# Six weight slots in two sizes, down halves behind the fifth product, a norm shift from three tiles

## The chip, the cores and the metric

The kernel runs on one core of a Trainium2 chip. Its engines are named as in the profile: PE (TensorE matmul; PEld is its weight load), DVE (VectorE), ACT (ScalarE), POOL (GpSimd) and SP (SyncE, which issues nearly all DMAs here). The metric is device time of one launch in microseconds. Before the change it is 1253.96 us, the median of three runs (1253.59 to 1255.86).

## The reference, cut to what matters

Two request groups (a prompt of 512 positions and a sample of 32) go through two layers that share their weights, 544 columns in all; the model is 1024 wide.

```python
for l in range(DEPTH):                       # 2 layers
    z = x @ w_in                             # one projection, split among three mixers
    a = gmlp(z); b = latent_attention(z); c = rg_lru(z)
    x = layer_norm(ALPHA * x + concat(a, b, c) @ w_o)        # first norm
    up = x @ w_up                            # 1024 -> 2 * 2816
    g, v = split(causal_dwconv3(up))
    x = layer_norm(ALPHA * x + (gelu(g) * v) @ w_down)       # second norm
```

All of it is fp32, and the caches and states are outputs too.

## The kernel before

**Layout and arithmetic.** Activations lie transposed: eight tiles `xT` of 128 features by 544 columns. Each product is made of three fp32r matmuls (lines 88 to 91): both operands are split into a high part (ACT rounds it) and a low part (DVE subtracts it), and high x high, high x low and low x high are summed. A PSUM bank holds half the columns, 272, so every product runs in two halves `hv`.

**Weights.** A raw weight tile is loaded by SP into one of four slots `wr` (line 94), and split into a high and a low tile in the slots `wh` and `wl`, five of each, 1024 columns wide (lines 102 to 112, and `pair` in `forms`). Some tiles next to a norm go to pages of 512 columns instead (`page_weights`, line 223). A split can't start before a slot is free, and a slot is free when the last matmul on its tile has run.

**Stages of a layer.** The mixer projects with tiles of w_in: latent weights in three tiles `wkv`, then `wuqr`, two gate tiles `wga0` and `wga1`, and so on (lines 330 to 470). `wo_stage` runs w_o's eight tiles through `proj_ln`: the tiles 0 and 1 together, then one by one; for the last three both halves are put apart, and the first two up tiles are split to slots meanwhile (`pre_up`, line 1039), so that the norm's first half can be done while PE runs the last second halves.

**The feed-forward** (`ffn`, line 1086) has 22 units, each a gate tile and a value tile of 128 features, in four column blocks `BLK` of 6, 4, 5 and 7 units. In the first block a unit is two plain projections, 96 matmuls. The other blocks use seven products of half size in place of eight (`seven`, line 1147), 84 matmuls a unit: the differences of the activations are the four pairs `TX`, made once by `mixed_x` while the first block runs (`settle`, line 1094), those of the weights are made for each unit by `forms` (line 1047): splits A11 and A12 (`fa`), S3 and S1 (`fb`), S2 and S4 (`fc`), each 1024 columns, and A22 (`fd`), 512. The gated result of a unit is split into two pages whose pool `FPT` names by block and unit: `g` for pages `pg`, `p` for `pp`, `t` for `pt`.

**Down products.** After each block its part of w_down runs: eight tiles, two halves each, 16 halves. For the first three blocks these are the generator `late`, and the next block pulls from it: `seven` stops after its second and after its fifth product, and the halves of that unit are shared between the two places (lines 1200 to 1207). A tile's weights are loaded and split when its first half is pulled. The last block's down product runs in `proj_ln` with the second norm.

**The norm** (`LN`, line 842) shifts by a mean before squaring: when the first four tiles are summed into `lns`, PE sums over partitions (line 886), ACT copies the mean, DVE subtracts it from all eight tiles, and the squares of tiles 1 to 3 are added in the shift, those of later tiles as they arrive. `stats` and `apply` then make the normed tiles, half by half; for the kernel's last norm four tiles are put apart instead of three, and the output is stored from there.

**Order.** The program is written as one sequence; a planner puts each engine's instructions in order ahead of the launch, by its own estimate of when operands and slots are there, and adds the semaphores. Engines then run their queues in that order.

Of the kernel before, what the change touches and what calls it, by code (L numbers as in the profile page):

```python
# [8 lines left out]
F32R = mybir.dt.float32r  # L9
AF = mybir.ActivationFunctionType  # L10
ALU = mybir.AluOpType
# [8 lines left out]
HW = 272  # L20
# [2 lines left out]
PG = 550  # L23
D_FF = 2816
NI = 22
BLK = ((0, 6), (6, 4), (10, 5), (15, 7))
FPT = ("", "ggpp", "", "ggppp")
KO = (0, 2, 4, 6, 1, 3, 5, 7)
ALPHA = (2.0 * DEPTH) ** 0.25
SCALE = 96 ** -0.5  # L30
# [16 lines left out]
def trunk_kernel(ctx: ExitStack, tc: tile.TileContext, i, o, k):  # L47
# [1 line left out]
    pool = ctx.enter_context(tc.tile_pool(name="sb", bufs=1))  # L49
    psum = ctx.enter_context(tc.tile_pool(name="ps", bufs=1, space=bass.MemoryType.PSUM))  # L50
    dram = ctx.enter_context(tc.tile_pool(name="dr", bufs=1, space=bass.MemoryType.DRAM))
    BUFS = dict(pg=28, pt=12, kb=8, pp=8, wr=4, wh=5, wl=5)

    def page(name, dt=F32, tag="pg"):
        return pool.tile([128, W if tag == "pp" else PG], dt, tag=tag, name=name, bufs=BUFS[tag])
# [38 lines left out]
    def load_w(src, kk, cols, name):  # L94
        wr = pool.tile([128, kk, cols], F32, tag="wr", name=name + "r", bufs=BUFS["wr"])
        nc.sync.dma_start(out=wr, in_=src)
        return wr
# [1 line left out]
    def raw_page(name):  # L99
        return pool.tile([128, 512], F32, tag="wr", name=name, bufs=BUFS["wr"])  # L100

    def split_w(wr, kk, cols, name):
        wh = pool.tile([128, kk, cols], F32R, tag="wh", name=name + "h", bufs=BUFS["wh"])
        wl = pool.tile([128, kk, cols], F32R, tag="wl", name=name + "l", bufs=BUFS["wl"])
        with ExitStack() as st:
            for ins in gate:
                st.enter_context(tc.issue_after(ins.ins))
            split(wh, wl, wr)
        return wh, wl

    def weights(src, kk, cols, name):
        return split_w(load_w(src, kk, cols, name), kk, cols, name)

    def rsqrt(y, v, t):
        a = act(y, v, AF.Abs_reciprocal_sqrt)
# [95 lines left out]
        return [[b[:, 0:HW] for b in r] for r in bs]  # L211


    def col_weights(src, kk, name, kper=8):
        res = []
        for c in range(0, kk, kper):
            n = min(kper, kk - c)
            wh, wl = weights(src[:, 128 * c:128 * (c + n)].rearrange("p (k c) -> p k c", k=n), n, 128, name)
            for j in range(n):
                res.append((wh, wl, j))  # L220
        return res
# [618 lines left out]


    class LN:
        def __init__(self, xT, first_op, va, cg, cb, spill, final, ns, tag):
            self.x, self.op, self.va, self.cg, self.cb = xT, first_op, va, cg, cb
            self.spill = spill
            self.final = final
            self.n1 = 8 - ns
            self.tag = tag

        def warm(self):  # L850
            t = const([128, 1], F32, "warm")
# [16 lines left out]
        def gather(self, m, c):  # L868
            if m == 0:
                return  # L870
            if m == 1:
                self.s = page("lns", tag=self.tag)[:, 0:W]
                tt(self.s, self.x[0][:, 0:W], self.x[1][:, 0:W], ALU.add)
                return
            s = self.s[:, c]
            tt(s, s, self.x[m][:, c], ALU.add)
            if m >= 4:
                self.square(m, c)

        def shift(self):  # L880
            s = self.s
            c = self.c = page("lnc", tag=self.tag)[:, 0:W]
            q = self.q = page("lnq", tag=self.tag)[:, 0:W]
            for h in HV:
                b = bank("lnm", "ss")
                nc.tensor.matmul(b[:, 0:HW], ones, s[:, h], start=True, stop=True)
                act(c[:, h], b[:, 0:HW], AF.Copy, scale=1.0 / 512)
            for m in (4, 0, 1, 2, 3, 5, 6, 7):
                x = self.x[m][:, 0:W]
                tt(x, x, c, ALU.subtract)  # L890
                if m == 0:
                    act(q, x, AF.Square)
                elif m in (1, 2, 3):
                    self.square(m, slice(0, W))
            stt(s, c, -4.0, s, ALU.mult, ALU.add)

        def square(self, m, c):
            t = page("lnt", tag="kb")[:, c]
# [66 lines left out]

    def proj(wsrc, kts, evac, name):
        for m in range(8):
            w = col_weights(wsrc(m), len(kts), f"{name}{m}")
            for hv in range(2):
                evac(m, hv, mms([w], kts, hv)[0])  # L970
                yield

    def proj_ln(wsrc, kts, ln, name, kper, pre, mid, ko=None):
        n1 = ln.n1
        ns = 8 - n1

        def get(m):
            w = col_weights(wsrc(m), len(kts), f"{name}{m}", kper)
            return [w[j] for j in ko] if ko else w

        for ms in ((0, 1), (2,), (3,)):
            ws = [get(m) for m in ms]
            for hv in range(2):
                for m, ps in zip(ms, mms(ws, kts, hv)):
                    ln.evac(m, hv, ps)
            if ms[0] == 0 and mid is not None:
                mid()
        def one(m, w, hv):
            ps = mms([w], kts, hv)[0]
            if m == 4 and hv == 0:  # L990
                ln.shift()
            ln.evac(m, hv, ps)

        for m in range(4, n1):
            w = get(m)
            for hv in range(2):
                one(m, w, hv)
        ws = [get(m) for m in range(n1, 8)]
        nxt = pre() if pre is not None else None
        for j in range(ns):  # L1000
            one(n1 + j, ws[j], 0)
            if j == 0:
                ln.warm()
        for j in range(ns):
            ps = mms([ws[j]], kts, 1, (lambda: ln.stats(0)) if j == 0 else ln.head if ln.final and j == ns - 1 else None, 5)[0]
            if j == 0 and not ln.final:
                ln.apply(0, range(4))
            ln.evac(n1 + j, 1, ps)
        if ln.final:
            ln.stats(1)  # L1010
            ln.apply(0)
        else:
            ln.apply(0, range(4, 8))

        def hook():
            if not ln.final:
                ln.stats(1)
            ln.apply(1)
        rest = [] if ln.final else [lambda m=m: ln.settle(m) for m in range(8)]
        return nxt, hook, rest  # L1020

    def wo_stage(l, va, pre):
        xT = []
        for m in range(8):
            x = page(f"xT{m}")
            nc.sync.dma_start(out=x[:, 0:W], in_=xd[l][m])
            if m >= 4:
                act(x[:, 0:W], x[:, 0:W], scale=ALPHA)
            xT.append(x)
        ln = LN(xT, "alpha", va, C_LN1G, C_LN1B, None, False, 3, "pp")  # L1030
        ko = [6, 7, 2, 3, 0, 4, 1, 5]

        kts = [KX[m] for m in ko]
        return xT, *proj_ln(lambda m: i["wo"][l, m], kts, ln, "wo", 8, pre, None, ko)
# [12 lines left out]
    def forms(l, i_):  # L1047
        w = [load_w(i["wup"][l, NI * s + i_].rearrange("p (k c) -> p k c", k=8), 8, 128, "wup") for s in range(2)]
        (a11, a12), (a21, a22) = [(r[:, 0:4, :], r[:, 4:8, :]) for r in w]

        def pair(n):
            return [pool.tile([128, n, 128], F32R, tag=t, name=f"wf{t}", bufs=BUFS[t]) for t in ("wh", "wl")]

        fa, fb, fc, fd = pair(8), pair(8), pair(8), pair(4)
        split(*fa, w[0])
        split(*fd, a22)
        tt(a22, a21, a22, ALU.add)
        tt(a21, a11, a21, ALU.subtract)
        tt(a11, a22, a11, ALU.subtract)
        tt(a12, a12, a11, ALU.subtract)  # L1060
        split(*fb, w[1])
        split(*fc, w[0])
        return dict(A11=(fa, 0), A12=(fa, 4), A22=(fd, 0), S3=(fb, 0), S1=(fb, 4), S2=(fc, 0), S4=(fc, 4))
# [22 lines left out]
    def ffn(l, va, vf, xT, first, hook, rest, pre):  # L1086
# [14 lines left out]
        for bl, (i0, nk) in enumerate(BLK):  # L1101
# [95 lines left out]
            if bl == 0:  # L1197
                for tl in tiles[done:]:
                    unit(tl)
            for j in range(nk if bl else 0):  # L1200
                mix = seven(i0 + j)
                n = 16 * (j + 1) // nk - 16 * j // nk
                for c in ((n + 1) // 2, n // 2):
                    next(mix)
                    for _ in range(c):
                        next(late)
                next(mix, None)
# [3 lines left out]

            if bl < len(BLK) - 1:
                def ev2(m, hv, ps, bl=bl):
                    x = xT[m][:, HV[hv]]
                    if bl == 0:
                        stt(x, x, ALPHA, ps, ALU.mult, ALU.add)
                    else:
                        tt(x, x, ps, ALU.add)
                late = proj(wsrc, [fts[j] for j in sorted(fts)], ev2, "wd")
            else:  # L1220
                fin = l == DEPTH - 1

                def mid():
                    nc.sync.dma_start(out=o[7][l], in_=fo)

                ln = LN(xT, "add", va, C_LN2G, C_LN2B, o[0] if fin else xd[l + 1], fin, 4 if fin else 3, "pg")
                nxt = proj_ln(wsrc, [fts[j] for j in sorted(fts)], ln, "wd", 8, pre, mid)
        return nxt

# [134 lines left out]
```

## Time and profile before

| | us |
|---|---|
| median of three runs | 1253.96 |
| the profiled execution | 1253.95 |
| its span, first to last instruction | 1252.1 |
| PE busy | 1223.2 (98%) |
| DVE busy | 1013.6 (81%) |
| ACT busy | 741.4 (59%) |
| mean granted TensorE clock | 0.995 |

Matmuls are pipelined and their ends are modelled, so PE's busy share says little of its pace; the distance between two starts does. "Idle before" is the time an engine stood still ahead of an instruction, with what ended it. The chain that ended last is PE for 82% of the span, DVE for 8% and ACT for 7%.

### The profile page before, as it was taken

The page shows a single profiled execution, that of the slowest core. Times are in us where ns is not written, and L with a number is a line of the kernel's source. Part 1 is how long each engine was busy: PE and PEld are TensorE (multiplying, and loading weights), DVE is VectorE, ACT ScalarE, POOL GpSimd, SP SyncE. Part 2 cuts the span into 40 slices and gives each one's busy share as a digit, 9 for nine tenths or more (in the row PEclk, how much of TensorE's full clock was granted, in tenths as well). Part 3 has the DMA queues.
Part 4 walks back from the last instruction along what each step waited for, and adds up shares of the span by engine and source line. Part 5 has one row for each costly group of instructions (what it writes and reads, how often), then busy time and mean ns, then how long its engine had stood idle before and what let it go on. Part 6 is the DMA issues. An engine that isn't in the chain of part 4 may idle for free.

```text
span 1252.1 us, 24029 instructions
## 1 busy us (share of the span) xinstructions
PE 1223.2 (98%) x9305; PEld 1178.7 (94%) x9305; DVE 1013.6 (81%) x1932; ACT 741.4 (59%) x1616; POOL 45.7 (4%) x222
## 2 busy tenths in 40 slices
PE   9999999999999999999899999999999999999994
PEld 9999879999999999999899997899999999999994
DVE  6766977997788889886886767689968788898858
ACT  6485874496455655553465767646955455565633
POOL 2400000000000000000000100000000000000000
PEclk9999999999999999999999999999999999999998
DMA  8243434022232332325144423340213223323312
GB/s 284 75 141 98 125 104 161 18 86 72 73 110 83 95 98 89 100 77 170 46 147 136 118 85 113 118 136 18 94 60 105 65 93 93 106 83 106 114 36 73
DMA packets 51043, 125.16 MB, mean 100 GB/s; under 512 B 7784, under 2 KB 13928, under 8 KB 50928
## 3 DMA queue, kind: packets, MB, share of 16 engines
q1 hardware_dynamic: 50928, 123.62, 31.8%
q8 instruction: 73, 1.20, 0.4%
q14 instruction: 42, 0.34, 0.1%
HBM read 113.17 MB, written 5.97 MB: 95 GB/s over the span
## 4 chain that ended last, share of the span: by engine, by line
PE 82%; DVE 8%; ACT 7%; issue 1%; DMA 0%; SPq 0%; ACTq 0%; DVEq 0%
PE mm L89 22%; PE mm L90 21%; PE mm L91 21%; ACT wfwh L64 2%; PE ov L255 2%; DVE xT L70 2%; ACT ac L64 1%; PE ol L255 1%; PE pT L132 1%; ACT xp L64 1%; DVE ac L70 1%; PE s L89 1%; DVE wupr L67 1%; DVE xT L67 1%; PE kv L396 1%
## 5 line engine op out<-in xcount | busy, mean ns | idle before, releaser
L64 ACT ACTIVATE wfwh<-wupr 128x1024 fp32r<-128x1024 f32 (+1 forms) x128 | 121.7, 951 | 122.6 <-PE mm L90 66.1
L67 DVE TENSOR_TENSOR wfwl<-wupr,wfwh 128x1024 fp32r<-128x1024 f32 (+1 forms) x128 | 139.4, 1089 | 14.3 <-ACT wfwh L64 13.0
L89 PE MATMUL mm<-th,wfwh 128*128 128x272 f32 x512 | 148.4, 291 | 0.0
L90 PE MATMUL mm<-tl,wfwh 128*128 128x272 f32 x512 | 147.4, 288 | 0.0
L91 PE MATMUL mm<-th,wfwl 128*128 128x272 f32 x512 | 146.4, 288 | 0.0
L70 DVE SCALAR_TENSOR_TENSOR ac<-xp,vf,ac 128x544 f32<-128x544 f32 x176 | 136.1, 781 | 8.0 <-ACT xp L64 7.2
L90 PE MATMUL mm<-xl,wfwh 128*128 128x272 f32 x384 | 111.1, 289 | 0.0
L91 PE MATMUL mm<-xh,wfwl 128*128 128x272 f32 x384 | 111.1, 289 | 0.0
L89 PE MATMUL mm<-xh,wuph 128*128 128x272 f32 x384 | 109.5, 291 | 1.5 <-DVE xT L67 1.5
L89 PE MATMUL mm<-xh,wfwh 128*128 128x272 f32 x384 | 110.9, 289 | 0.0
L90 PE MATMUL mm<-xl,wuph 128*128 128x272 f32 x384 | 110.3, 289 | 0.0
L91 PE MATMUL mm<-xh,wupl 128*128 128x272 f32 x384 | 110.3, 288 | 0.0
L89 PEld LDWEIGHTS mm<-th,wfwh 128*128 128x128 f32 x512 | 96.3, 188 | 1.2 <-ACT u L64 0.8
L90 PEld LDWEIGHTS mm<-tl,wfwh 128*128 128x128 f32 x512 | 96.6, 189 | 0.0
L91 PEld LDWEIGHTS mm<-th,wfwl 128*128 128x128 f32 x512 | 96.3, 189 | 0.0
L67 DVE TENSOR_TENSOR wupr<-wupr 128x512 f32<-128x512 f32 x128 | 88.2, 689 | 2.4
L89 PEld LDWEIGHTS mm<-xh,wuph 128*128 128x128 f32 x384 | 71.7, 188 | 2.3 <-DVE xT L67 1.9
L91 PEld LDWEIGHTS mm<-xh,wfwl 128*128 128x128 f32 x384 | 72.4, 189 | 0.0
L90 PEld LDWEIGHTS mm<-xl,wuph 128*128 128x128 f32 x384 | 72.4, 189 | 0.0
L89 PEld LDWEIGHTS mm<-xh,wfwh 128*128 128x128 f32 x384 | 72.4, 188 | 0.0
L90 PEld LDWEIGHTS mm<-xl,wfwh 128*128 128x128 f32 x384 | 72.3, 188 | 0.0
L91 PEld LDWEIGHTS mm<-xh,wupl 128*128 128x128 f32 x384 | 72.3, 188 | 0.0
(517 smaller groups left out, 4006.9 us busy)
## 6 DMA issues: line engine op xcount, KB each, us to landing
wupr<-in_wup_dram SPq DMA_DIRECT2D x88, 512.0 KB
xT<-in_x_dram SPq DMA_DIRECT2D x14, 272.0 KB
xd<-xT SPq DMA_DIRECT2D x8, 272.0 KB
xT<-xd SPq DMA_DIRECT2D x8, 272.0 KB
out_dram<-xT SPq DMA_DIRECT2D x16, 136.0 KB
ckT<-in_ckT_dram SPq DMA_DIRECT2D x8, 256.0 KB
cr<-in_ck_dram SPq DMA_DIRECT2D x8, 256.0 KB
win0r<-in_win_dram SPq DMA_DIRECT2D x8, 192.0 KB
```

The source lines that it names most:

```text
L64: return nc.scalar.activation(out=out, in_=in_, func=func, **kw)
L67: return (e or nc.vector).tensor_tensor(out=out, in0=a, in1=b, op=op)
L70: return nc.vector.scalar_tensor_tensor(out=out, in0=a, scalar=s, in1=b, op0=op0, op1=op1)
L89: nc.tensor.matmul(ps, lh, rh, start=start, stop=False, **kw)
L90: nc.tensor.matmul(ps, lh, rl, start=False, stop=False, **kw)
L91: lastmm[0] = nc.tensor.matmul(ps, ll, rh, start=False, stop=stop, **kw)
L132: nc.tensor.transpose(out, in_, ident[0:p, 0:p])
L255: nc.tensor.matmul(ps, a, b, start=start, stop=stop)
L396: nc.tensor.matmul(b[0:n, 0:288], XL[j][:, cs], wh[:, ci, :], start=False, stop=False)
```

## The change

The column blocks become 5, 5, 5 and 7 units. The five slots `wh`, `wl` become four (tag `w`), and two slots `vh`, `vl` of 640 columns are added (tag `v`): for A22 and for the down tiles of the first three blocks. Pages `pp` go from eight to seven, and the fifth unit of the second block keeps its result in `pt`. In the late blocks one half is pulled after the second product and the others after the fifth; the number of halves up to a unit's end is odd, but for the last. The second norm's shift is taken from the first three tiles, the first norm's still from four.

```diff
-BLK = ((0, 6), (6, 4), (10, 5), (15, 7))
-FPT = ("", "ggpp", "", "ggppp")
+BLK = ((0, 5), (5, 5), (10, 5), (15, 7))
+FPT = ("", "ggppt", "", "ggppp")
-    BUFS = dict(pg=28, pt=12, kb=8, pp=8, wr=4, wh=5, wl=5)
+    BUFS = dict(pg=28, pt=12, kb=8, pp=7, wr=4, wh=4, wl=4, vh=2, vl=2)
-    def split_w(wr, kk, cols, name):
-        wh = pool.tile([128, kk, cols], F32R, tag="wh", name=name + "h", bufs=BUFS["wh"])
-        wl = pool.tile([128, kk, cols], F32R, tag="wl", name=name + "l", bufs=BUFS["wl"])
+    def split_w(wr, kk, cols, name, tag="w"):
+        wh, wl = [pool.tile([128, kk, cols], F32R, tag=tag + p, name=name + p, bufs=BUFS[tag + p]) for p in "hl"]
...
-            if m >= 4:
+            if m >= self.n0:
                 self.square(m, c)
...
-                act(c[:, h], b[:, 0:HW], AF.Copy, scale=1.0 / 512)
-            for m in (4, 0, 1, 2, 3, 5, 6, 7):
+                act(c[:, h], b[:, 0:HW], AF.Copy, scale=1.0 / (128 * n0))
+            for m in (n0, *range(n0), *range(n0 + 1, 8)):
...
-                elif m in (1, 2, 3):
+                elif m < n0:
                     self.square(m, slice(0, W))
-            stt(s, c, -4.0, s, ALU.mult, ALU.add)
+            stt(s, c, -float(n0), s, ALU.mult, ALU.add)
...
     def proj(wsrc, kts, evac, name):
-            w = col_weights(wsrc(m), len(kts), f"{name}{m}")
+            w = col_weights(wsrc(m), len(kts), f"{name}{m}", tag="v")
...
-        for ms in ((0, 1), (2,), (3,)):
+        n0 = ln.n0
+        for ms in ((0, 1), (2,), (3,))[0:n0 - 1]:
...
-            if m == 4 and hv == 0:
+            if m == n0 and hv == 0:
                 ln.shift()
...
-        for m in range(4, n1):
+        for m in range(n0, n1):
...
         def pair(n):
-            return [pool.tile([128, n, 128], F32R, tag=t, name=f"wf{t}", bufs=BUFS[t]) for t in ("wh", "wl")]
+            w = "v" if n == 4 else "w"
+            return [pool.tile([128, n, 128], F32R, tag=w + p, name=f"wf{p}", bufs=BUFS[w + p]) for p in "hl"]
...
+            halves = 0
             for j in range(nk if bl else 0):
                 mix = seven(i0 + j)
-                n = 16 * (j + 1) // nk - 16 * j // nk
-                for c in ((n + 1) // 2, n // 2):
+                end = 16 if j == nk - 1 else 2 * round(8 * (j + 1) / nk - 0.5) + 1
+                for c in (1, end - halves - 1):
                     next(mix)
+                    halves += c
                     for _ in range(c):
                         next(late)
```

With these counts a unit's two pulls are 1 and 2, 1 and 3, 1 and 1, 1 and 3, 1 and 2 halves in a block of five units; in the block of seven they are 1 and 2 in the first and the last unit and 1 and 1 between.

## Rows read from the trace of the kernel before

**Rows 1.** The page's busy line of PE: busy us, share, instructions.
```profile
PE 1223.2 (98%) x9305; PEld 1178.7 (94%) x9305; DVE 1013.6 (81%) x1932; ACT 741.4 (59%) x1616; POOL 45.7 (4%) x222
```
**Rows 2.** Stretches: length; busy of PE, PEld, DVE, ACT, POOL (count); clock; DMA; GB/s.
```profile
207.30:226.00 18.70, 18.70 (x147) 18.54 (x147) 18.62 (x33) 10.40 (x18) 0.10 (x1) 1.00 0.39 134
233.00:307.25 74.25, 73.52 (x582) 73.12 (x581) 67.07 (x120) 56.99 (x137) 1.16 (x12) 1.00 0.19 61
307.25:386.00 78.75, 78.64 (x626) 78.40 (x625) 60.41 (x90) 39.40 (x77) 0.69 (x7) 1.00 0.26 78
465.10:572.10 107.00, 105.98 (x831) 104.51 (x830) 94.28 (x141) 63.97 (x136) 1.84 (x17) 1.00 0.34 102
```
**Rows 3.** PE's waits: what waited, for what; total us, times, longest.
```profile
PE mm L89 <- ACT wd3h L64: 1.8, 4, 0.6
...
PE mm L89 <- ACT wd2h L64: 0.6, 2, 0.3
```
**Rows 4.** Order of time in the last block: start, us, engine, instruction [idle before].
```profile
482.75 0.29 PE L91 MATMUL mm<-xh,wfwl 128*128 128x272 f32 x1
483.36 0.39 PE L89 MATMUL mm<-fh,wd1h 128*128 128x272 f32 x1 [0.32 <-ACT wd1h L64]
...
483.71 0.29 PE L89 MATMUL mm<-th,wfwh 128*128 128x272 f32 x1
...
482.77 0.33 SPq L96 DMA_DIRECT2D wd2r<-in_wdn_dram  x1
...
497.45 0.73 ACT L64 ACTIVATE wd2h<-wd2r 128x640 fp32r<-128x640 f32 x1
...
499.28 0.82 DVE L67 TENSOR_TENSOR wd2l<-wd2r,wd2h 128x640 fp32r<-128x640 f32 x1
```
**Rows 5.** Order of time at layer 0's second norm: DVE, ACT, DVE, PE.
```profile
589.79 1.08 DVE L67 TENSOR_TENSOR wd7l<-wd7r,wd7h 128x896 fp32r<-128x896 f32 x1
...
597.43 1.28 ACT L64 ACT_TABLE_LOAD   x1
...
599.34 3.27 DVE L67 TENSOR_TENSOR xT<-xT,lnc 128x544 f32<-128x544 f32 x5 [3.08 <-ACT lnc L64]
...
616.57 0.29 PE L91 MATMUL mm<-fh,wd7l 128*128 128x272 f32 x1
620.78 0.40 PE L89 MATMUL mm<-xh,win0h 128*128 128x272 f32 x1 [3.92 <-ACT xh L64]
```
**Rows 6.** Stretches at the same place, columns as in rows 2.
```profile
599.34:620.78 21.44, 17.52 (x137) 17.08 (x135) 21.24 (x46) 8.29 (x18) 0.00 (x0) 1.00 0.16 42
621.10:624.40 3.30, 3.30 (x16) 3.06 (x15) 3.30 (x10) 2.18 (x5) 0.00 (x0) 0.50 0.00 0
```
**Rows 7.** Order of time at the kernel's end: DVE, PE, DVE.
```profile
1216.75 3.27 DVE L67 TENSOR_TENSOR xT<-xT,lnc 128x544 f32<-128x544 f32 x5 [4.21 <-ACT lnc L64]
...
1236.16 0.47 PE L908 MATMUL ln<-lns,ones 128*128 128x272 f32 x1 [1.94 <-DVE lns L67]
...
1242.52 4.62 DVE L70 SCALAR_TENSOR_TENSOR xT<-xT,va,lnc 128x272 f32<-128x272 f32 x11
```
**Rows 8.** Order of time at layer 0's first norm: DVE, then PE's first up product.
```profile
202.42 1.22 DVE L67 TENSOR_TENSOR wo7l<-wo7r,wo7h 128x1024 fp32r<-128x1024 f32 x1
203.55 1.29 DVE L67 TENSOR_TENSOR wupl<-wupr,wuph 128x512 fp32r<-128x512 f32 x2
...
220.18 1.21 DVE L67 TENSOR_TENSOR wupl<-wupr,wuph 128x1024 fp32r<-128x1024 f32 x1
...
226.95 0.79 DVE L70 SCALAR_TENSOR_TENSOR xT<-ln,xT 128x272 f32<-128x272 f32 x2 [0.89 <-ACT lnt L64]
...
233.04 0.41 PE L89 MATMUL mm<-xh,wuph 128*128 128x272 f32 x2
```
**Rows 9.** Order of time at layer 0's gate tiles: PE, DVE.
```profile
53.51 0.29 PE L91 MATMUL mm<-xh,wga0l 128*128 128x272 f32 x1
...
54.98 1.21 DVE L67 TENSOR_TENSOR wga1l<-wga1r,wga1h 128x1024 fp32r<-128x1024 f32 x1
```

More of the change, by code (lines that the diff above doesn't have):

```diff
@@ L109, in split_w, with weights @@
         return wh, wl
-    def weights(src, kk, cols, name):
-        return split_w(load_w(src, kk, cols, name), kk, cols, name)
+    def weights(src, kk, cols, name, tag="w"):
+        return split_w(load_w(src, kk, cols, name), kk, cols, name, tag)
     def rsqrt(y, v, t):
@@ L211, in first_units, with col_weights @@
         return [[b[:, 0:HW] for b in r] for r in bs]
-    def col_weights(src, kk, name, kper=8):
+    def col_weights(src, kk, name, kper=8, tag="w"):
         res = []
@@ L217, in col_weights @@
             n = min(kper, kk - c)
-            wh, wl = weights(src[:, 128 * c:128 * (c + n)].rearrange("p (k c) -> p k c", k=n), n, 128, name)
+            wh, wl = weights(src[:, 128 * c:128 * (c + n)].rearrange("p (k c) -> p k c", k=n), n, 128, name, tag)
             for j in range(n):
@@ L842, in trunk_kernel, with __init__ @@
     class LN:
-        def __init__(self, xT, first_op, va, cg, cb, spill, final, ns, tag):
+        def __init__(self, xT, first_op, va, cg, cb, spill, final, ns, tag, n0):
             self.x, self.op, self.va, self.cg, self.cb = xT, first_op, va, cg, cb
@@ L848, in __init__ @@
             self.tag = tag
+            self.n0 = n0
         def warm(self):
@@ L876, in gather @@
             tt(s, s, self.x[m][:, c], ALU.add)
-            if m >= 4:
+            if m >= self.n0:
                 self.square(m, c)
         def shift(self):
-            s = self.s
+            s, n0 = self.s, self.n0
             c = self.c = page("lnc", tag=self.tag)[:, 0:W]
@@ L1029, in wo_stage @@
             xT.append(x)
-        ln = LN(xT, "alpha", va, C_LN1G, C_LN1B, None, False, 3, "pp")
+        ln = LN(xT, "alpha", va, C_LN1G, C_LN1B, None, False, 3, "pp", 4)
         ko = [6, 7, 2, 3, 0, 4, 1, 5]
@@ L1224, in mid @@
                     nc.sync.dma_start(out=o[7][l], in_=fo)
-                ln = LN(xT, "add", va, C_LN2G, C_LN2B, o[0] if fin else xd[l + 1], fin, 4 if fin else 3, "pg")
+                ln = LN(xT, "add", va, C_LN2G, C_LN2B, o[0] if fin else xd[l + 1], fin, 4 if fin else 3, "pg", 3)
                 nxt = proj_ln(wsrc, [fts[j] for j in sorted(fts)], ln, "wd", 8, pre, mid)
```

## The prediction

> **What bounds the kernel now.** I read the page's busy line first, then the stages by stretches, then PE's waits, then the engines in order of time around each wait. PE is busy for 98% of the span [rows 1], so what isn't fewer matmuls must be a wait of PE or the tail. The stretches of layer 0 [rows 2] give the pace: the column block of 307.25 to 386.00 runs 626 matmuls in 78.75 us, 0.126 each, and nearly no wait; VectorE (DVE) fills 60.4 of it, but 94.3 of 107 us in the last block. PE's waits name the rest. The weights of the down halves hold it ten times (five per layer, wd3 four times, the others two each); the first and the last of the four groups are in [rows 3], and all four sum to 4.4 us, counted from the modelled end of the matmul before. By starts one such wait costs more: 482.75 to 483.71 is three steps and takes 0.96, where three take 0.375 [rows 4], so 0.59. Six of the ten cost that, three 0.83 and one 1.05 by their starts: 7.1 us. Beside these there are two norm stalls: at the layer boundary PE starts nothing from 616.57 to 620.78 [rows 5], and runs at half clock (0.50, the 1.2 GHz level) for 3.3 us soon after [rows 6]; at the end it waits 1.94 us, and DVE then works until 1247.1 [rows 7]. The sum below stands on the profiled execution: 1253.95 us, 1.85 outside its span, and 0.01 from the median of the runs.
>
> **The change part by part.**
>
> *Column 5 by seven products.* A gated unit costs 2 tiles x 2 halves x 8 x 3 = 96 matmuls in the first block and 7 x 4 x 3 = 84 in the others. One unit per layer moves: 2 x 12 = 24 fewer, at 0.125 us: **-3.0 us**. The down products stay 22 units x 48 in all. ScalarE and DVE get one and a half more splits and four 512-column differences for it; these run beside PE. Block 0 loses two tiles (12 us of PE, and on DVE two splits, four taps, a product and a split), and keeps all four mixed pairs. DVE was busy there for 67.1 of 74.25 us [rows 2], so it gets tighter; its slack is at the block's end, where the new first forms fall. I take 0; without this cover it costs up to one split per form set, three of 1.2 us each (as wo7's, [rows 8]), 3.7 per layer; below nothing it can't go, as nothing there waits on block 0 now.
>
> *Down halves.* Now one half runs after the second product, and it is nearly always the second half of a tile whose weights are there; the others come after the fifth product, three products (36 matmuls, 4.5 us) later. So the split needn't be ready behind A11, where the waits are. The load isn't late: wd2's was issued at 482.77, its split ran at 497.45 for 0.73 us and the low part at 499.28 for 0.82 [rows 4]; SP's queue issues the same loads, cut from 768 and 512 columns to 640. What is late next: with two slots of 640, one is A22's until the seventh product. Where the second of two tiles is begun in the same unit as the first is ended (three times each in the first two late blocks, once in the last: 14 in all), its split waits for the half just run or for A22. Ends: -7.1 when no wait is left; 0 as the most that simply isn't recovered (beyond that is a rival). The order on PE already puts `th,wfwh` products between pieces of a half [rows 4], which covers one split; I take the nearer end, less 0.15 us for each of the 14: **-5.0**.
>
> *Norm shift after three tiles (second norm of a layer).* Mean, copies and subtractions start one tile of down products earlier: 42 matmuls, 5.2 us. The count of subtractions, squares and sums stays. Layer boundary: DVE stood idle for 3.08 us until 599.34, as an ACT table load of 1.28 falls between the two copies of the mean [rows 5], and from there DVE is full until PE restarts [rows 6]. Started at 594.1, it fills these 3.08, but four slots push wd7's low split (1.08, [rows 5]) into the same stretch: -2.0, ends 0 and -4.2 (the whole stall). The half clock came after the long stall: 16 matmuls in 3.3 us [rows 6] where 2.0 would do, so 1.3; with half the stall left I count half of it. Together **-2.7**, ends 0 and -5.5. The end of the kernel: DVE idles 4.21 us before the subtractions [rows 7]; less wd7's 1.08 is 3.1. It stays full to the last, so its end moves by that, until PE's end binds: three of the last 11 scalings, 1.3 us, then lie ahead of PE's end, and the 1.94 of waiting goes, 3.2 in all. **-3.0**, ends 0 and -3.2.
>
> *Four slots of 1024 instead of five.* First norm: wo5, wo6, wo7 and two up tiles are alive together, five. So each split from wo4 on is one tile, 48 matmuls or 6.0 us, later: wo7's low part (1.22 at 202.42), and the page splits that wait for its raw buffer (1.29 at 203.55), come after 207 [rows 8], where DVE is busy for 18.62 of 18.70 us [rows 2]. The second up tile's low part (1.21 at 220.18) must wait for wo5's second half, which ends two halves, 6.0 us, before the first up product at 233.04: at 227.0, inside the norm's last chain instead of before it [rows 8]. Later work 2.5, less 0.5 of the idle 0.89 before 226.95 [rows 8]: the first up product waits 2.0 longer. Twice: **+4.0**; ends 0 (the planner finds other gaps) and 2 x 3.7 (the up split counts too).
>
> Mixer: the three latent weights and wuqr fill four slots until the latent products end, so the first gate tile (wga0) must be split where wga1 is now: its low part at 54.98, done at 56.19, while the third gate matmul wants it at 53.51 [rows 9]. At most 2.7, at least 0 (DVE takes it first); I take one low split, 1.2, per layer: **+2.4**. Elsewhere in the mixer and attention tiles are split long before use, and pages `pp` (7 for 8) hold two heads' six: 0.
>
> Sum: -3.0 - 5.0 - 2.7 - 3.0 + 4.0 + 2.4 = -7.3, so 1253.95 - 7.3 = **1246.6 us**. Ends of this sum: 1235 (all gains, no costs) to 1271 (no gain but the matmuls, and all costs, block 0's cover gone too).
>
> **Rivals.**
>
> *A. The slots never bind.* The planner finds gaps for every later split, and no half waits: -3.0 - 7.1 - 2.7 - 3.0 gives 1238.2. For it: in the mixer most splits run many us before use. Against: five tiles are alive at the first norm by the code.
>
> *B. The second tile's split holds PE (slower).* At those 14 places PE's program has the half straight behind the one that frees the slot. Each then costs the high split 0.73, the low 0.82 and a hand-over, less two matmuls: about 1.6. 14 x 1.6 = 22 in place of the ten old waits: 1253.95 - 2.3 - 7.1 + 22 = 1266.5 (the -2.3 are the other terms). It decides from 0.85 each, where the time passes 1256.5. For it: nothing overtakes on PE; `th,wfwh` at 483.71 needs no wd1 and still starts after it [rows 4]. Against: halves are already cut apart by other products in the planned order. The Trainium skill, TensorE: Matmul & The Clock Gate, section The mechanism, says matmuls keep strict program order; the rows agree, so this hangs on the planned order alone.
>
> *C. The slots cost their upper ends (no change).* Every displaced split lands just ahead of what PE waits for: 7.4 at the first norms and 5.4 at the gates in place of 4.0 and 2.4, so 1253.95 - 7.3 + 6.4 = 1253.1. For it: PE waits today where a weight is split late [rows 3], and DVE has no room at the first norm [rows 2]. Against: DVE idles 0.89 there [rows 8] and takes splits in planned order, not last. The Trainium skill, Perfetto Trace Analysis, section Optimization Strategy, says that one gap repeated on the engine that should be full can mean too little room to allocate the next tile; by it a cut from five slots to four would bring such gaps to every stage that fills five, which is this rival's time.
>
> **How the numbers follow.** Forecast 0.58, A 0.17, B 0.10, C 0.15. This kernel's measurement tells about 0.2%, 2.5 us, from no change: faster is below 1251.4, slower above 1256.5. Faster: 0.55 of the forecast, all of A, 0.04 of C: 0.76. Same: 0.03 of the forecast, 0.10 of C: 0.13. Slower: 0.10 of B, 0.01 of C: 0.11. The range leaves out B, the far half of A and a little of each side: 1238 to 1254; the forecast alone lies in 1241 to 1251.
>
> **What would show it.** 24 fewer matmuls. No wait of PE for wd splits behind A11; if instead waits for wd stand behind another down half, B holds. The first shift subtraction some 5 us earlier against its down products at both places, PE's gap at the boundary near 2 us, the half clock gone or not. A gap of 2 us before the first up products, and the low split of the second up tile inside the norm's chain; one before the third gate matmul. If the first two gaps are missing, A is right; if the tail from the last down matmul to the end stays at 18 us, the norm term is wrong.

## The result, and the profile after

The changed kernel takes **1399.53 us** (median of four runs, 1395.26 to 1402.50) beside 1254.1 for the kernel before on the same chip: ratio 1.1156, 95% interval 1.1126 to 1.1186. The forecast was 1246.6, the range 1238 to 1254.

The page of the changed kernel, its busy line and its chain by engine; before, see [rows 1]:
```profile
PE 1273.8 (91%) x9281; PEld 1208.8 (87%) x9281; DVE 1018.6 (73%) x1950; ACT 747.3 (54%) x1616; POOL 45.7 (3%) x222
...
PE 68%; DVE 18%; ACT 9%; issue 4%; DMA 1%; DVEq 0%; ACTq 0%
```
The 24 matmuls are gone, and DVE and ACT have about the work they had; yet PE falls from 98% to 91%, and the chain goes through DVE and ACT much more often. So nothing was added: something waits. PE's waits (what waited for what; total us, times, longest), where [rows 3] named down weights:
```profile
PE mm L89 <- ACT wfh L64: 84.5, 56, 1.8
PE mm L89 <- ACT xh L64: 10.4, 3, 4.1
PE mm L89 <- ACT wd0h L64: 5.7, 4, 1.4
...
PE mm L91 <- DVE wga0l L67: 1.3, 2, 0.8
```
The waits for wd1, wd2, wd3 and wd6 behind A11 are gone. In their place stands one that the kernel before did not have: PE waits for `wfh`, a split of the up weights' forms, in the units of the late blocks. (The four waits named `wd0h`, 1.4 us each, stand at the same place, in the first units of the last two blocks: by starts PE has 30 such waits in layer 0, in 16 of its 17 late units.) By stretches of the changed kernel (length; busy of PE, PEld, DVE, ACT, POOL; clock; DMA; GB/s): layer 0's late blocks to the next layer, one unit from its first product to the next one's, and 3 us inside it:
```profile
300.23:690.13 389.90, 342.07 (x2495) 329.63 (x2493) 270.75 (x422) 178.38 (x361) 5.62 (x41) 0.96 0.25 80
...
583.67:603.47 19.80, 16.63 (x117) 15.98 (x116) 13.31 (x20) 9.35 (x21) 0.20 (x2) 0.91 0.21 70
592.90:595.90 3.00, 3.00 (x15) 3.00 (x14) 3.00 (x5) 0.81 (x2) 0.00 (x0) 0.50 0.65 194
```
The late blocks and one unit in the kernel before, with one unit fewer in the late blocks:
```profile
307.31:620.78 313.47, 307.09 (x2411) 303.65 (x2409) 262.04 (x406) 168.80 (x345) 4.81 (x39) 1.00 0.32 95
...
479.85:494.73 14.88, 14.56 (x117) 14.33 (x115) 13.43 (x21) 8.90 (x20) 0.20 (x2) 1.00 0.30 94
```
The loss sits in the late blocks of both layers, 17 units each. One unit takes 19.80 us instead of 14.88 for the same 117 recorded matmuls. About 3.2 us of that is idle, and for some 3 us TensorE runs at half clock (0.50, the 1.2 GHz level) behind the two waits: 15 matmuls in 3.00 us where 24 would go.

Why the split is late shows in the unit ahead of that one (565.33 to 583.67, 18.34 us), engine by engine, in order of time (start, us, instruction, idle before). PE of the changed kernel:
```profile
565.09 0.28 PE L90 MATMUL mm<-tl,wfh 128*128 128x272 f32 x1
565.21 0.29 PE L91 MATMUL mm<-th,wfl 128*128 128x272 f32 x1
565.33 0.29 PE L91 MATMUL mm<-xh,wfl 128*128 128x272 f32 x1
...
569.85 0.29 PE L91 MATMUL mm<-fh,wd3l 128*128 128x272 f32 x1
571.78 0.39 PE L89 MATMUL mm<-th,wfh 128*128 128x272 f32 x1 [1.65 <-ACT wfh L64]
...
572.26 0.29 PE L90 MATMUL mm<-fl,wd4h 128*128 128x272 f32 x1
574.08 0.39 PE L89 MATMUL mm<-th,wfh 128*128 128x272 f32 x1 [1.53 <-ACT wfh L64]
```
ACT beside it:
```profile
565.42 0.62 ACT L64 ACTIVATE wfh<-wupr 128x512 fp32r<-128x512 f32 x1
...
570.05 0.74 ACT L64 ACTIVATE wd4h<-wd4r 128x640 fp32r<-128x640 f32 x1
570.69 1.04 ACT L64 ACTIVATE wfh<-wupr 128x1024 fp32r<-128x1024 f32 x1
572.37 0.66 ACT L64 ACTIVATE fh<-ac 128x544 fp32r<-128x544 f32 x1 [0.64 <-DVE ac L67]
572.97 2.01 ACT L64 ACTIVATE wfh<-wupr 128x1024 fp32r<-128x1024 f32 x2
```
DVE beside it, the low part of A22 and the four differences:
```profile
566.07 0.69 DVE L67 TENSOR_TENSOR wfl<-wupr,wfh 128x512 fp32r<-128x512 f32 x1 [1.53 <-ACT wfh L64]
567.38 0.68 DVE L67 TENSOR_TENSOR wupr<-wupr 128x512 f32<-128x512 f32 x1
569.72 0.68 DVE L67 TENSOR_TENSOR wupr<-wupr 128x512 f32<-128x512 f32 x1
571.02 0.68 DVE L67 TENSOR_TENSOR wupr<-wupr 128x512 f32<-128x512 f32 x1
572.25 0.68 DVE L67 TENSOR_TENSOR wupr<-wupr 128x512 f32<-128x512 f32 x1
```
Read it backwards. PE starts nothing from 569.85 to 571.78 and from 572.26 to 574.08, until the splits of S3/S1 (570.69, ends 571.73) and of S2/S4 (572.97, ends 574.03) are there. S2/S4 needs the fourth difference (572.25 + 0.68 = 572.93); S3/S1 needs the second (ends 570.40, while ACT is on wd4 until 570.7). The first difference overwrites raw A22, so all four come after the split of A22: the 512-column `wfh` at 565.42. That split starts 0.05 us after the last matmul that reads the high part of the *previous* unit's A22 (565.09 + 0.28 = 565.37). In the kernel before, the same step of ACT:
```profile
489.91 0.63 ACT L64 ACTIVATE wfwh<-wupr 128x512 fp32r<-128x512 f32 x1 [0.92 <-PE mm L90]
...
493.07 1.06 ACT L64 ACTIVATE wfwh<-wupr 128x1024 fp32r<-128x1024 f32 x1 [2.29 <-DVE wupr L67]
```
There the A22 split runs when the fifth product ends, 4.8 us before the unit's first product (494.73); in the changed kernel it is 0.1 us behind it (565.33). So from this pair of traces, theory 1: two narrow slots hold this unit's A22 and an unfinished down tile; the next unit's A22 waits for the first, and the differences and both other splits queue behind it. The split's row doesn't name this wait: it shows no idle time, as ACT is busy with other work until then. So the theory needs a test.

The places that were forecast, in the changed kernel: the first up product, DVE's last low split of up weights ahead of it, the third gate matmul, the layer boundary, and the first subtraction of the last norm's shift ([rows 5, 7 to 9]):
```profile
237.21 0.52 PE L89 MATMUL mm<-xh,wuph 128*128 128x272 f32 x2 [4.06 <-ACT xh L64]
...
227.69 1.23 DVE L67 TENSOR_TENSOR wupl<-wupr,wuph 128x1024 fp32r<-128x1024 f32 x1
...
54.61 0.39 PE L91 MATMUL mm<-xh,wga0l 128*128 128x272 f32 x1 [0.76 <-DVE wga0l L67]
...
690.13 0.39 PE L89 MATMUL mm<-xh,win0h 128*128 128x272 f32 x1 [2.31 <-ACT xh L64]
...
1355.17 3.27 DVE L67 TENSOR_TENSOR xT<-xT,lnc 128x544 f32<-128x544 f32 x5 [3.21 <-ACT lnc L64]
```

### The profile page after: what moved, and what is told of

It is laid out like the page before. It is cut to its first block, busy times and chain, and to the rows that moved or that the text cites. A ratio compares the mean times of both kernels' runs of the same rounds, so it can differ in the third digit from the quotient of the medians.

```text
span 1393.4 us, 23895 instructions
## 1 busy us (share of the span) xinstructions
PE 1273.8 (91%) x9281; PEld 1208.8 (87%) x9281; DVE 1018.6 (73%) x1950; ACT 747.3 (54%) x1616; POOL 45.7 (3%) x222
## 4 chain that ended last, share of the span: by engine, by line
PE 68%; DVE 18%; ACT 9%; issue 4%; DMA 1%; DVEq 0%; ACTq 0%
PE mm L89 19%; PE mm L91 18%; PE mm L90 17%; DVE ac L70 5%; DVE wupr L67 4%; ACT wfh L64 3%; DVE xp L67 2%; ACT ac L64 2%; DVE wfl L67 2%; PE ov L254 1%; DVE ac L67 1%; DVE xT L70 1%; ACT fh L64 1%; PE pT L131 1%; PE ol L254 1%
## 5 line engine op out<-in xcount | busy, mean ns | idle before, releaser
L89 PE MATMUL mm<-th,wfh 128*128 128x272 f32 x544 | 176.9, 325 | 90.2 <-ACT wfh L64 84.5
L67 DVE TENSOR_TENSOR wfl<-wupr,wfh 128x1024 fp32r<-128x1024 f32 (+1 forms) x136 | 148.0, 1088 | 47.3 <-ACT wfh L64 46.9
L91 PE MATMUL mm<-th,wfl 128*128 128x272 f32 x544 | 168.0, 313 | 0.3
L90 PE MATMUL mm<-tl,wfh 128*128 128x272 f32 x544 | 167.2, 307 | 0.0
L64 ACT ACTIVATE wfh<-wupr 128x1024 fp32r<-128x1024 f32 (+1 forms) x136 | 126.5, 943 | 19.0 <-PE mm L90 9.3
L89 PE MATMUL mm<-xh,wfh 128*128 128x272 f32 x408 | 118.9, 291 | 0.0
L90 PE MATMUL mm<-xl,wfh 128*128 128x272 f32 x408 | 118.9, 291 | 0.0
L91 PE MATMUL mm<-xh,wfl 128*128 128x272 f32 x408 | 117.7, 288 | 0.0
L91 PEld LDWEIGHTS mm<-th,wfl 128*128 128x128 f32 x544 | 114.4, 212 | 1.7 <-DVE wfl L67 1.6
L90 PEld LDWEIGHTS mm<-tl,wfh 128*128 128x128 f32 x544 | 113.6, 209 | 0.0
```

The lines of the kernel that those rows point to most:

```text
L64: return nc.scalar.activation(out=out, in_=in_, func=func, **kw)
L67: return (e or nc.vector).tensor_tensor(out=out, in0=a, in1=b, op=op)
L89: nc.tensor.matmul(ps, lh, rh, start=start, stop=False, **kw)
L90: nc.tensor.matmul(ps, lh, rl, start=False, stop=False, **kw)
L91: lastmm[0] = nc.tensor.matmul(ps, ll, rh, start=False, stop=stop, **kw)
```

## The experiments

Times are medians; the kernel before was timed beside each group, at 1254.0 to 1254.7 us.

**A22's product ahead of S4** (changed kernel):
```diff
+                product(b1, f["A22"], t[3])
                 product(b5, f["S4"], x[2])
...
-                product(b1, f["A22"], t[3])
```


> The changed kernel, with the product A22 put ahead of S4, so the 640-column slot that holds A22 comes free 12 matmuls (12 x 0.125 = 1.5 us) earlier in each of the 34 late units; no slot count and no half is moved. Theory 1 (the next unit's A22 split waits for this unit's A22, because the other narrow slot holds an unfinished down tile, and the four in-place differences of the weights stand behind that split, so S2 and S1 reach PE late): the stall of a unit, some 4.1 us, shrinks by 1.5, so 1399.5 - 34 x 1.5 = 1348, between 1340 and 1360. Rival 2 (four wide slots instead of five hold the splits for S3/S1 and S2/S4): no change, 1399. Rival 3 (with one half instead of two between A11 and S2, PE has too little to do while the forms are made): no change, 1399.

Measured: 1355.3 us, 44.2 less than the changed kernel, 1.30 for each of 34 units. ACT's waits, and the A22 split of one unit:
```profile
ACT wfh L64 <- PE mm L90: 59.9, 34, 2.5
```
```profile
543.22 0.63 ACT L64 ACTIVATE wfh<-wupr 128x512 fp32r<-128x512 f32 x1 [1.89 <-PE mm L90]
```
The wait is now named: splits of ACT wait for PE 34 times, and 32 of these are splits of A22 (58.4 of the 59.9 us), one in each unit but the first of each layer's late blocks. Theory 1 holds, with the time inside its range; rivals 2 and 3 wanted 1399.

**A22 in the wide slots** (changed kernel):
```diff
-            w = "v" if n == 4 else "w"
+            w = "w"
```


> The changed kernel, with A22 split to the four wide slots (as A11/A12, S3/S1 and S2/S4 are) and the two narrow slots left to the down tiles alone. Theory 1 (A22's split waits for the narrow slot): it can now take the slot of A11/A12, which is free after the second product, so most of the stall goes, 1245 to 1270. Rival 2 (too few wide slots): four forms on four slots instead of three on four, so the stall grows, above 1400. Rival 3 (too little PE work between A11 and S2): no change, 1399.

Measured: 1252.1 us, ratio to before 0.9983 (0.9974 to 0.9993). The wait for `wfh` is gone from PE's list, and the late blocks of layer 0 are back at full clock:
```profile
300.33:619.26 318.93, 316.44 (x2495) 314.04 (x2493) 274.02 (x422) 176.93 (x362) 5.63 (x41) 1.00 0.30 96
```
```profile
493.31 0.63 ACT L64 ACTIVATE wfh<-wupr 128x512 fp32r<-128x512 f32 x1 [0.92 <-PE mm L90]
```
One word changed, the same memory: 147.4 us. Not A11's slot, as expected, but again a slot that comes free at the fifth product (its matmuls run up to 493.11), as in the kernel before. Rival 2, too few wide slots, falls: four forms on four slots run well.

**All of the change but the slots** (blocks, halves and norm put into the kernel before; the diff is against the changed kernel and cut to one line, the tags `w` and `v` go with it):
```diff
-    BUFS = dict(pg=28, pt=12, kb=8, pp=7, wr=4, wh=4, wl=4, vh=2, vl=2)
+    BUFS = dict(pg=28, pt=12, kb=8, pp=8, wr=4, wh=5, wl=5)
```


> The kernel before with everything of the change but the slots: blocks of 5, 5, 5 and 7 units, one half behind the second product and the rest behind the fifth, norm shift after three tiles; five slots of 1024 columns for all splits, eight pages pp. Theory 1 and rival 2 (both are of the slots): the stalls of 4 us a unit are gone, 1243 to 1252. Rival 3 (the place of the halves): the stalls stay, near 1399.

Measured: **1241.1 us**, ratio 0.9895 (0.9880 to 0.9910), and 1241.4 in a second group. Layer 0's late blocks:
```profile
295.62:614.88 319.26, 316.56 (x2494) 313.93 (x2493) 272.18 (x423) 178.22 (x363) 5.15 (x42) 1.00 0.31 99
```
This beats both kernels; a simpler one that does as well is below. Rival 3, the place of the halves, falls with it: the halves lie as in the changed kernel, and the late blocks take within 0.4 us what they take with A22 in the wide slots.

**An even number of halves up to each unit's end** (changed kernel):
```diff
-                end = 16 if j == nk - 1 else 2 * round(8 * (j + 1) / nk - 0.5) + 1
+                end = 2 * round(8 * (j + 1) / nk)
```


> The changed kernel with an even number of down halves up to each unit's end (one behind the second product, the rest behind the fifth, as before): a down tile begun behind the second product is ended behind the fifth, so its narrow slot is free before S4 and A22 run, 24 matmuls or 3.0 us before A22's own. Theory 1: the next unit's A22 split takes that slot, and the stall shrinks by some 3.0 us a unit, to 1399.5 - 34 x 3.0 = 1298, between 1270 and 1320. Rival 2 and rival 3: no change, near 1399, as neither the wide slots nor the number of halves between A11 and S2 is touched.

Measured: 1364.8 us, a gain of 34.7 and not 100: the direction was right, the size missed. ACT, then PE, of two units:
```profile
551.38 0.63 ACT L64 ACTIVATE wfh<-wupr 128x512 fp32r<-128x512 f32 x1 [0.75 <-PE mm L90]
...
572.75 0.63 ACT L64 ACTIVATE wfh<-wupr 128x512 fp32r<-128x512 f32 x1 [4.37 <-PE mm L90]
```
```profile
558.88 0.36 PE L89 MATMUL mm<-th,wfh 128*128 128x272 f32 x1 [1.45 <-ACT wd3h L64]
```
In a unit of two halves the A22 split is early (551.38, 2.9 us before the unit's first product at 554.25), but PE then waits for wd3. By the code's order the new down tile is left with the slot that A22 leaves at the unit's end; that this slot is what made wd3 late isn't shown. In a unit of four halves two down tiles pass through, and ACT stands idle for 4.37 us ahead of A22's split, until PE is through with the second. So with two slots for three tenants an even count moves the wait and doesn't end it.

**A22 loaded a second time**, so that the differences need not wait for its split (changed kernel):
```diff
-        split(*fd, a22)
+        again = pool.tile([128, 4, 128], F32, tag="wr", name="wupa", bufs=BUFS["wr"])
+        nc.sync.dma_start(out=again, in_=...)    # the A22 quarter of the value tile
+        split(*fd, again)
```


> The changed kernel, slots as they are, but the A22 quarter of the weights is loaded a second time to a raw slot of its own, and its split reads that copy; so the four in-place differences no longer stand behind the A22 split (44 more loads of 256 KB on SP). The split itself still waits for the narrow slot. Theory 1 (the waits come by way of the differences): S3/S1 and S2/S4 are ready in time, and A22 is wanted only at the seventh product, so most of the 147 us over the kernel with A22 in wide slots goes: 1250 to 1275. Rival (the narrow slot alone is short, and A22's product waits as long as S1 did): the stall moves to the seventh product and the time stays within 30 us of 1399. Rival 2 (raw slots: a third raw tile per unit on four slots makes the loads late): 1300 to 1400, with PE's waits ended by a DMA or by splits that waited for one.

Measured: 1259.5 us, ratio 1.0040 (1.0026 to 1.0054); the loads are 34, one a unit, not 44. ACT:
```profile
512.77 1.06 ACT L64 ACTIVATE wfh<-wupr 128x1024 fp32r<-128x1024 f32 x1 [1.24 <-DVE wupr L67]
...
517.33 0.63 ACT L64 ACTIVATE wfh<-wupa 128x512 fp32r<-128x512 f32 x1
```
The A22 split still comes late, now 4.6 us *after* the split of S3/S1, and nobody minds: A22 is wanted only by the seventh product. 140 of the 147 us go although no slot was added. So the price was not the late split itself but what stood behind it, the four in-place differences and the two splits made from them.

**The norm's shift alone** (kernel before, with the lines of the change's diff in `LN` and `proj_ln` that use the count):
```diff
-                ln = LN(xT, ..., fin, 4 if fin else 3, "pg")
+                ln = LN(xT, ..., fin, 4 if fin else 3, "pg", 3)
```


> The kernel before with only the second norm's shift taken after three tiles instead of four; slots, blocks and halves as before. By the prediction's terms, -2.7 at the layer boundary and -3.0 at the end: 1254.0 - 5.7 = 1248.3. Rival (at the boundary the last weights' split and the table load of ACT, not the shift, set the chain): only the end's -3.0, 1251.

Measured: 1248.1 us, ratio 0.9947 (0.9934 to 0.9959), -6.6. The first subtraction at layer 0's boundary, and 3.2 us after it:
```profile
595.03 3.27 DVE L67 TENSOR_TENSOR xT<-xT,lnc 128x544 f32<-128x544 f32 x5 [3.21 <-ACT lnc L64]
```
```profile
619.20:622.40 3.20, 3.16 (x24) 2.94 (x24) 3.20 (x9) 2.08 (x5) 0.00 (x0) 1.00 0.00 0
```
The shift starts 22.4 us before the last down matmul (617.40), where it was 17.2 before. PE's gap falls from 4.21 to 1.58, and the half clock of [rows 6] is gone: 24 matmuls in 3.20 us at 1.00.

**The halves alone** (kernel before): the loop of the change's diff, nothing else.


> The kernel before with only the down halves moved: one behind the second product, the rest behind the fifth, an odd number up to a unit's end; five slots, blocks 6, 4, 5, 7. By the prediction's term -5.0 with ends -7.1 and 0: 1249.0, between 1247 and 1254; the ten waits for down weights gone from PE's waits. Rival (the second tile's split holds PE where two tiles meet behind the fifth product): 1254 or more, with waits for down weights behind other halves.

Measured: 1248.1 us, ratio 0.9946 (0.9932 to 0.9960), -6.6. No wait for a down weight is left in PE's list, and layer 0's late blocks take 3.27 us less than before:
```profile
307.03:617.23 310.20, 305.97 (x2410) 303.50 (x2408) 260.75 (x406) 169.13 (x345) 4.84 (x39) 1.00 0.32 97
```

**The blocks alone** (kernel before): the two lines `BLK` and `FPT`.


> The kernel before with only the column blocks 5, 5, 5 and 7 (and the fifth unit of the second block in pt pages); slots, halves and norm as before. By the prediction's term 24 fewer matmuls of 0.125: 1254.0 - 3.0 = 1251.0. Rival (the first block no longer covers what VectorE does in it): 1254, with PE waiting in or behind the first block.

Measured: 1255.8 us, ratio 1.0007 (0.9998 to 1.0016): no gain. Layer 0's first block and its late blocks, and two of PE's waits:
```profile
232.61:294.85 62.24, 61.49 (x487) 61.09 (x486) 59.91 (x112) 48.82 (x118) 0.86 (x9) 1.00 0.15 45
294.85:620.80 325.95, 318.88 (x2494) 314.28 (x2492) 273.54 (x423) 177.59 (x364) 5.11 (x42) 1.00 0.32 97
```
```profile
PE mm L89 <- ACT wd3h L64: 2.0, 6, 0.3
...
PE mm L89 <- ACT wd6h L64: 1.3, 4, 0.3
```
The first block falls by 12.03 us, 96 matmuls, as worked out. The late blocks grow by 12.48 where 84 matmuls would be 10.5: there are more waits for wd3 and wd6 (6 and 4 where 4 and 2 were in the whole kernel), and one where the first block ends.

**Norm and halves without the blocks**, and **all but the slots again** beside it:


> The kernel before with the norm shift after three tiles and the down halves moved; blocks 6, 4, 5, 7 and five wide slots as before. The two parts alone gave -6.6 each: if they touch different waits, 1254.4 - 13.2 = 1241.2. Theory (the blocks' 24 fewer matmuls were eaten by new waits for down weights only as long as halves stood behind A11): the kernel with all but the slots is 3.0 us faster than this one, so this one is near 1244. Rival (the blocks' matmuls are given back somewhere else): both are alike within 1 us, 1241.

> The kernel with all of the change but the slots once more, beside the kernel with the norm and the halves alone: 1241.1 as before; the difference of the two is what the blocks are worth when the halves don't wait.

Measured: 1241.0 and 1241.4 us, ratios 0.9893 (0.9878 to 0.9908) and 0.9895 (0.9882 to 0.9909): alike. So the medians show no gain of the blocks here either, and the rival holds: the simplest kernel that beats both leaves out slots and blocks. PE of the kernel with the blocks:
```profile
300.49 0.40 PE L89 MATMUL mm<-fh,wd0h 128*128 128x272 f32 x1 [0.31 <-ACT fh L64]
...
382.46 0.39 PE L89 MATMUL mm<-th,wfwh 128*128 128x272 f32 x1 [0.82 <-DVE xp L67]
```
Two waits per layer that the kernel without the blocks does not have, 0.47 and 0.99 us by starts, take back most of the 1.5 us per layer (the first block and the late blocks together are 0.27 us shorter in layer 0 and 0.50 in layer 1): one where the shorter first block ends (its last result's split is late for the first down half), one where the second block ends.

**Even halves with five wide slots:**


> The kernel with all but the slots, with an even number of halves up to a unit's end, five wide slots. Theory 1 (the number of halves matters only by which narrow slot is free): now like the odd order, 1241, within 2 us. Rival (an even order makes the half behind the second product wait for its tile's split, as behind A11 in the kernel before): some of the ten waits come back, 1244 to 1249, with waits of PE for wd splits behind A11.

Measured: 1253.2 us, ratio 0.9992 (0.9983 to 1.0001): 12 us slower than the odd order, beyond the rival's range. PE's waits:
```profile
PE mm L89 <- ACT wd6h L64: 5.2, 6, 1.2
PE mm L89 <- ACT wd7h L64: 2.4, 2, 1.2
PE mm L89 <- ACT wd3h L64: 2.1, 6, 0.5
```
With an even count the half behind the second product begins a new tile, so its split is late behind A11 as in [rows 3]. The gain of the halves hangs on the odd count, not on the place alone; and the parity matters by itself, against what theory 1 was stretched to say.

**Both norms after three tiles** (all but the slots, and 3 for the first norm):
```diff
-        ln = LN(xT, "alpha", va, C_LN1G, C_LN1B, None, False, 3, "pp", 4)
+        ln = LN(xT, "alpha", va, C_LN1G, C_LN1B, None, False, 3, "pp", 3)
```


> The kernel with all but the slots, and the first norm's shift after three tiles too. PE's longest gap at the first norm is about 1.0 us twice in the kernel with all but the slots: if the earlier shift lets the norm's first half end sooner, -1 to -2, 1239 to 1240. Rival (VectorE is full from the shift to the first up product, so an earlier start only moves work ahead of the last tiles' sums): no change, 1241, or slower by a us.

Measured: 1241.0 us, beside 1241.4 without: no change, as the rival had it. The outputs lie up to 0.020 (relative) from the reference, so this is a measurement of time and no proposal.

## Why the prediction failed, by its own steps

The account in medians: 1254.1, less 13.0 for all but the slots, plus 11.0 for four wide slots, two narrow ones for the down tiles alone and one page `pp` fewer (1252.1 against 1241.1), plus 147.4 for A22 in the narrow slots: 1399.5.

*The step that failed* is "What is late next: with two slots of 640, one is A22's until the seventh product. Where the second of two tiles is begun ..., its split waits for the half just run or for A22." The tenants were right, the waiter was wrong. I asked only who of the down tiles waits for A22, priced that at 0.15 in 14 places, and did not ask for whom the *next* A22 waits, nor what is queued behind its split. With an odd count a down tile lives on over every unit's end but a block's last, so the two slots are full there, and the next A22 can start only after the seventh product. (At a block's end it is no better: ACT waits 1.92 us there, until 400.58, for the last half of wd7, which PE runs last in the unit.) Behind it stand four differences of 0.68, mixed with the unit's taps on DVE, and two splits of 1.04. Rival B named the place (the narrow slots) and the side (slower), at 14 x 1.6 = 22 us; the real one is 4.3 on the average of 34 units, and no wait for a down weight stands behind another half, which was B's sign. No rival had this chain, and the range, built from the bounds of the terms named, could not hold it. Without the chain the change comes to 1252.1: inside the range, but near rival C's 1253.1 and not near the forecast's 1246.6.

*The layer's arithmetic of the loss.* The late blocks of layer 0 take 389.90 us with A22 in the narrow slots and 318.93 without: 71.0, over 17 units 4.2 each. By PE's starts it comes apart: some 50 us are the 30 waits, 13 are half clock (nine bouts of 12 to 15 matmuls at 0.23 instead of 0.125), and 8 are single steps of 0.15 to 0.45 us, of which the changed kernel has 97 and the other 29.

*24 matmuls, -3.0.* They are gone (9305 to 9281), but by the medians the time is not: +1.1 alone, +0.4 within the set, which is within the spread of the runs. "Block 0: I take 0" was the wrong end of its own bound (up to 3.7 per layer); the new waits are 1.46 per layer, at the ends of the first two blocks.

*Down halves, -5.0.* Right, a little low: -6.6 alone, near the end of -7.1. No second tile's split holds PE with five wide slots, so the 0.15 for each of 14 was not needed.

*Norm, -2.7 and -3.0.* Right in sum: -6.6 alone. The stages give -2.76 up to the boundary, -1.19 behind it (the half clock went whole, not half) and -2.13 in the tail (16.03 us from the last down matmul to the end, before 18.16). Its working had one flaw: DVE still idles 3.21 ahead of the subtractions; the whole chain moved earlier instead of filling that hole. In the changed kernel itself the gap is 2.59 by starts, near the 2 that was forecast, and the half clock stays; the tail is 14.75, 3.4 less than before.

*First norm, +4.0; gates, +2.4.* The mechanism is right, the first size is not: from w_o's first matmul to the first up product it takes 54.61 us in layer 0 and 54.31 in layer 1 with A22 in the wide slots, 50.08 each before, so 8.8 in all, above the upper end of 7.4 and most of the 11.0; I had counted one late low split in the norm's chain, but the loads of the up weights go out later too (SP's first at 197.49, before at 188.56), and four page splits (0.69 each, the first at 223.88) fall in there ahead of 227.69, which the kernel before had done by 211.9. The gates' wait came where it was forecast (0.76 idle at 54.61, and 0.53 in layer 1), but its price of 2.4 isn't seen: from the first matmul of the mixer to w_o's first, layer 0 takes 177.92 us with A22 in the wide slots and 177.95 before, layer 1 179.71 and 179.27. So a wait of PE in the middle of the mixer was nearly no loss at its end; what sets that end isn't shown. The rule of the Trainium skill that the prediction put beside rival C (Perfetto Trace Analysis, section Optimization Strategy: one gap repeated on the engine that should be full can mean too little room for the next tile) agrees with this trace, 60 waits of the same form; but not a byte was lacking, as A22 in the wide slots of the same memory has none of them, and the price was not the rival's 6 us but 147.

## What to carry to other kernels

When buffers are split into classes, list for each class its tenants at the moment of handover, and for each tenant what is queued behind its first write; the costly one may be the tile that is itself needed last. A step that overwrites its input in place ties everything behind it to the slot of whoever still has to copy that input: copying the input, or letting it draw on another class, gave back 140 and 147 us here. And a gain counted in fewer instructions is worth the stage's length after the change, not the count: 24 matmuls bought nothing that the medians show.

## What was not expected of the hardware

Behind some pairs of waits within one unit (1.9 and 1.5 to 1.8 us by starts) the granted clock fell to 0.50, for 12 to 15 matmuls: nine times in layer 0, which has 14 such pairs, and nine times in layer 1. In the other five units of layer 0 with such a pair (565.33 to 583.67 is one) it stayed at 1.00; what tells the two apart these traces don't show. At the boundary between the layers the clock stayed at 1.00 behind a wait of 1.58 us and fell behind 4.21 and, in the changed kernel, 2.59:
```profile
691.80:695.00 3.20, 3.20 (x16) 3.20 (x15) 3.16 (x10) 2.97 (x5) 0.00 (x0) 0.50 0.01 3
```
Sixteen matmuls there take the 3.20 us in which the kernel with the norm's shift alone ran 24.
